# Attention's constant rows and first queries: which rows the products take, and which engine writes and loads them

## The chip, the cores and the metric

The kernel runs on one core of a Trainium2 chip. The metric is the device time of one execution in microseconds (us). Before the change it was 2974.33 us, the median of three runs (2973.43 to 2976.23). The engines are TensorE (PE; its weight loads are counted apart as PEld), VectorE (DVE), ScalarE (ACT), GpSimd (POOL) and SyncE (SP), which issues most of the DMA transfers.

## The reference: what is computed

One layer of a hybrid trunk over 2064 tokens (2048 and 16 meta tokens) of width 1024. One input projection feeds three groups side by side: an RG-LRU recurrence, a forgetting attention of 8 heads with 64 columns each, and an RWKV-7 recurrence. Their outputs are projected back, and a feed-forward layer of width 2816 follows. The change is in the attention, which is

```python
c = jnp.cumsum(log_f, axis=1).transpose(0, 2, 1)
...
s = jnp.einsum('bhqd,bhkd->bhqk', qb, kh).astype(jnp.float32) + (cb[..., :, None] - c[..., None, :])
s = jnp.where(kpos[None, :] <= qpos[:, None], s, -jnp.inf)
p = jax.nn.softmax(s, axis=-1)
return jnp.einsum('bhqk,bhkd->bhqd', p.astype(vh.dtype), vh)
```

`c` is the running sum of the logarithms of the forget gates; a score is a product of query and key, plus the difference of `c` at the two places.

## The kernel before

The program runs in stages: the input projection (products L177 to L179 into `psp`), with the recurrences taken in small steps beside it; then attention (class `Attn`); then the output projection (`pswo`), the feed-forward layer's two products (`psu`, `psd`). The last RWKV and RG-LRU blocks are not through when the projection ends, at about 860 us, so they lie beside the first attention heads. The names of these recurrence steps in the trace: `rwxu`, `rwrav`, `rwwa`, `rwgt`, `rww`, `rstate` are RWKV's tiles; L1330 and L1361 multiply with the state `rstate`, which DVE copies at L1334 for the next step of the chain, four times in a row for one block; L1366 follows it; `rwraw` (L1034) is a piece of the projection's output that SP loads for the next part, and L1044/L1045 (ACT, then DVE) mix it with its neighbour token.

The order in which each engine takes its instructions is decided by a scheduler, when the program is built, from the program's order and a model of the durations. On the chip each engine then takes its list strictly in that order, and SP's DMA issues too: an instruction that waits holds back everything behind it on its engine.

Attention runs over two halves, of the query blocks 0 and 1 and then 2 and 3 (512 queries each), and within a half over the 8 heads. Keys and queries are kept as a high and a low part. For one head and block:

- `keys()` (L521) loads with SP. `k1` holds the keys' high part in rows 0 to 63 and the low part in rows 64 to 127. `k2` holds the high part in rows 0 to 63 (L537), a row of ones in row 64, and the two parts of `c`, `ch` and `cl`, in rows 65 and 66 (L539, L540). The other rows are zeros.
- `maxima()` (L552) loads the queries with SP: `q3` (L563), `q1` twice (L564, L565), `q2` (L566). `q3` has zeros in row 64 and ones in rows 65 and 66. The product `mx` of `q3` and `k2` (L576) with the triangle of L578 gives scores, whose greatest value DVE finds for each query (L581, into `mc`, set by a memset at L569). They are brought into a row by transposes (L591), and ACT writes them into row 64 of `q2` (L592).
- `weights()` (L672) makes the scores in two products, `k1` with `q1` (L704) and `k2` with `q2` (L705), so that row 64 subtracts the maximum. ACT takes the exponential (L709), GpSimd cuts the triangle and adds up the sums (L711, L748), and the values are multiplied at L727.

Maxima have two banks in `mx()`, scores two. `q1`, `q2`, `q3` are rings of three tiles, `k1` and `k2` of two; a third `k2` is made by `rear()` when half 1 begins (L837 and on), in memory that the recurrences have left.

The constant rows of these tiles are written by `__init__` and `fixed()`: for a `q3` three DVE memsets (L491, L492, L493), for a `q2` one (L473), for a `k2` four DVE casts of 64 x 520 elements from a column of the identity matrix (L499). The meta tokens' own small attention, `meta()`, uses `fixed()` too, with eight rows of ones, and there GpSimd sets the keys' rows.

Of the kernel before, what the change touches and what calls it, by code (L numbers as in the profile page):

```python
# [8 lines left out]
F32 = mybir.dt.float32  # L9
# [23 lines left out]
class Core:  # L33


    def __init__(self, tc, ctx):
        self.tc = tc
        self.nc = tc.nc
        self.ctx = ctx
        self.uid = 0  # L40
        nc = self.nc
        self.const = ctx.enter_context(tc.tile_pool(name="const", bufs=1))
        self.ident = self.const.tile([P, P], F32, name="ident")
        make_identity(nc, self.ident[:])
        self.flip = 0
        self.root = self.apart = False
        self.turns = 0
# [315 lines left out]
KHALF = META + 8 * P  # L363
# [85 lines left out]
class Attn:  # L449
# [3 lines left out]


    ONES = 1

    def __init__(self, core, pool, psum, more, scr):
        self.core, self.pool, self.psum, self.more, self.scr = core, pool, psum, more, scr
        self.wide, self.bank, self.place, self.tail = False, 0, 0, False
        nc = self.nc = core.nc  # L460
        self.clock, self.later, self.serial, self.added = 0, [], 0, 0
        self.pending, self.loads, self.steps, self.beside = None, [], [], iter(())
        self.marks = {}


        self.turn = {"k": 1, "k2": 1, "q2": 0, "q3": 0}
        self.ring = {s: [] for s in self.turn}
        for i in range(self.AHEAD + 1):
            q3 = pool.tile([P, 512], F32R, tag=f"q3_{i}", name=core.n("q3"), bufs=1)
            self.fixed(q3, None, self.ONES)  # L470
            self.ring["q3"].append(q3)
            q2 = pool.tile([P, 512], F32R, tag=f"q2_{i}", name=core.n("q2"), bufs=1)
            nc.vector.memset(q2[64:128].bitcast(F32), 0.0)  # L473
            self.ring["q2"].append(q2)
            if i > 1:
                continue
            k1 = pool.tile([P, 2, KHALF], F32R, tag=f"k1_{i}", name=core.n("k1"), bufs=1)
            self.rear(pool, f"k2_{i}")
            v1 = pool.tile([P, 2, NKT // 2 + 1, 64], F32, tag=f"v1_{i}", name=core.n("v1"), bufs=1)
            self.ring["k"].append((k1, v1))  # L480

    def rear(self, pool, tag):
        k2 = pool.tile([P, 2, KHALF], F32R, tag=tag, name=self.core.n("k2"), bufs=1)
        self.fixed(None, k2, self.ONES)
        self.ring["k2"].append(k2)

    def fixed(self, q, k, ones):

        if q is not None:

            self.nc.vector.memset(q[64:128].bitcast(F32), 0.0)  # L491
            self.nc.vector.memset(q[64 : 64 + ones + 2].bitcast(F32), 1.0)  # L492
            self.nc.vector.memset(q[64 : 64 + ones].bitcast(F32), 0.0)  # L493
        if k is not None:
            if ones == 1:
                col = self.core.ident[64:128, 64:65]
                kf = k.rearrange("p h t -> p (h t)")
                for c in range(0, 2 * KHALF, KHALF // 2):
                    self.nc.vector.tensor_copy(kf[64:128, c : c + KHALF // 2], col.to_broadcast([64, KHALF // 2]))  # L499
            else:  # L500
                self.nc.gpsimd.memset(k[64:128].bitcast(F32), 0.0)
                self.nc.gpsimd.memset(k[64 : 64 + ones].bitcast(F32), 1.0)

    def next(self, s):
        self.turn[s] = (self.turn[s] + 1) % len(self.ring[s])
# [15 lines left out]
    def keys(self, h, nt):  # L521
# [15 lines left out]
        nc.sync.dma_start(k2f[0:64, :n], scr["kh"][r, :n])  # L537
        g = 64 + self.ONES
        nc.sync.dma_start(k2f[g : g + 1, :n], scr["ch"][h : h + 1, :n])  # L539
# [12 lines left out]
    def maxima(self, h, b, keys):  # L552

        nc, core, scr = self.nc, self.core, self.scr
        k1, k2, v1 = keys
        r = slice(64 * h, 64 * h + 64)
        t0, n, ref = META + 512 * b, 512, 4 * b
        qt = [(P * i, P, META + P * (4 * b + i)) for i in range(4)]
        ts = slice(t0, t0 + n)
        q3 = self.next("q3")  # L560
        q1 = self.t([P, 512], "q1", F32R, self.AHEAD + 1)
        q2 = self.next("q2")
        nc.sync.dma_start(q3[0:64, :n].bitcast(F32), scr["qh"][r, ts])  # L563
        nc.sync.dma_start(q1[0:64, :n].bitcast(F32), scr["qh"][r, ts])  # L564
        nc.sync.dma_start(q1[64:128, :n].bitcast(F32), scr["qh"][r, ts])  # L565
        nc.sync.dma_start(q2[0:64, :n].bitcast(F32), scr["ql"][r, ts])  # L566
        nq = len(qt)
        mc = self.t([P, 4, 5], "mc")
        nc.vector.memset(mc[:], NEG)  # L569
        for i, (qo, rows, prior) in enumerate(qt):  # L570
            for ci in range(len(MAX_CUTS) - 1):
                a, e = MAX_CUTS[ci], min(MAX_CUTS[ci + 1], prior + rows)
                if a >= e:
                    break
                ps, last = self.mx(), e == prior + rows
                nc.tensor.matmul(ps[:rows, : e - a], q3[:, qo : qo + rows], k2[:, a:e], start=True, stop=not last)  # L576
                if last:
                    nc.tensor.matmul(  # L578
                        ps[:rows, prior - a : e - a], core.identb[:], core.futureb[:], start=False, stop=True
                    )  # L580
                self.reduced = nc.vector.tensor_reduce(  # L581
                    mc[:rows, i, ci : ci + 1], ps[:rows, : e - a], axis=AX.X, op=ALU.max
                )
                yield None
        bias = self.t([P, NKT], "bias", bufs=self.AHEAD + 1)
        yield q1, q2, bias
        sh = self.t([P, 4], "sh")
        nc.vector.tensor_reduce(sh[:], mc[:], axis=AX.X, op=ALU.max)
        ps = self.mx()
        for i in range(nq):  # L590
            nc.tensor.transpose(ps[0:1, P * i : P * i + P], sh[:, i : i + 1], core.ident[:])  # L591
        nc.scalar.activation(q2[64:65], ps[0:1], AF.Identity, scale=-1.0, bias=core.ncref[:, ref, h : h + 1])  # L592
        nc.scalar.activation(
            bias[:], core.ccol[:, :, h], AF.Identity, scale=-1.0, bias=core.cref[:, ref, h : h + 1]
        )
        yield None
# [75 lines left out]
    def weights(self, h, b, keys, queries, fill):  # L672
# [6 lines left out]
        nc, core, scr = self.nc, self.core, self.scr  # L679
        k1, k2, v1 = keys  # L680
        q1, q2, bias = queries

        t0, n = META + 512 * b, 512
# [3 lines left out]
        ts = slice(t0, t0 + n)  # L687
# [4 lines left out]
        def group_scores(group):  # L692

            nonlocal done
            out = []
            for jj in range(0, len(group), 2):
                if done:
                    fill(min(1.0, (done + 2) / len(kt)))
                done += 2
                self.tick()  # L700
                for j, rows, c0, mw, mo in group[jj : jj + 2]:
                    w, ks = n - c0, P * j
                    ps = self.ps("sc", 2)
                    nc.tensor.matmul(ps[:rows, :w], k1[:, ks : ks + rows], q1[:, c0:n], start=True, stop=False)  # L704
                    self.scored = nc.tensor.matmul(  # L705
                        ps[:rows, :w], k2[:, ks : ks + rows], q2[:, c0:n], start=False, stop=True
                    )
                    p = self.pool.tile([P, 512], F32, tag="p", name=core.n("p"), bufs=self.NP)
                    last = nc.scalar.activation(p[:rows, :w], ps[:rows, :w], AF.Exp, bias=bias[:rows, j : j + 1])  # L709
                    if mw:  # L710
                        last = nc.gpsimd.affine_select(  # L711
                            out=p[:rows, :mw], in_=p[:rows, :mw], compare_op=ALU.is_ge, fill=0.0, base=mo,
                            pattern=[[1, mw]], channel_multiplier=-1,
                        )
                    out.append((p, last))
            return out
# [88 lines left out]
        for i, group in enumerate(groups):  # L805
            ps_ = group_scores(group)
            self.marks[h, b, i] = self.scored
            self.flush()
            self.pending = lambda a=(group, ps_, i == 0, i == len(groups) - 1): group_values(*a)
# [1614 lines left out]
```

## Time and profile before

| what | us |
|---|---|
| median of the runs | 2974.33 |
| time of the profiled execution | 2975.74 |
| its span, first to last instruction | 2974.0 |
| TensorE busy | 2852.4 |
| VectorE busy | 2039.5 |
| ScalarE busy | 1503.8 |
| GpSimd busy | 1285.9 |
| score products L704 and L705 start at | 873.70 and 884.52 |
| first reduce of maxima, L581 | 875.15 |
| first exponential, L709 | 885.40 |
| DVE's casts for the third k2 | 1094.9 to 1098.2 |

The mean granted clock of TensorE is 0.979 of its full speed. Times in rows are counted from the span's start. A row of a timeline or of the chain gives start, duration, engine, line and operation; a bracket behind it is the idle time just before it on its engine, with what ended it. A group's row gives count, least, median and greatest duration in ns, and the first and last start.

### The profile page before, as it was taken

What the parts mean: (1) busy time and instruction counts of PE and PEld (TensorE: products, weight loads), DVE (VectorE), ACT (ScalarE), POOL (GpSimd) and SP (SyncE); (2) the same over time, 40 slices, a digit from 0 to 9 for tenths busy, and PEclk for the clock granted to TensorE, in tenths of its full rate; (3) what the DMA queues carried; (4) which work ended last, traced back from release to release, by engine and by line L of the source; (5) the groups of instructions that cost most, each with busy time, mean ns of one, the idle gap of its engine ahead of it and who ended that gap; (6) DMA issues with size and microseconds to landing.
All of it is one profiled execution on the core that took longest, in us unless ns stands there. A gap on an engine that the chain in (4) does not pass through costs nothing.

```text
span 2974.0 us, 53306 instructions
## 1 busy us (share of the span) xinstructions
PE 2852.4 (96%) x18826; PEld 2444.3 (82%) x18826; DVE 2039.5 (69%) x3977; ACT 1503.8 (51%) x2937; POOL 1285.9 (43%) x1555
## 2 busy tenths in 40 slices
PE   6999999999988889999999999999999999999998
PEld 6998899888866555666568999999999999787887
DVE  5257754665677775566656998888778787646766
ACT  4246432554346655455644665666565665324333
POOL 1001121132114566667722667455655444646443
PEclk9999899999988999999999999999999999999999
DMA  6776479576653358445245665577777764436453
GB/s 216 237 231 220 144 250 320 182 245 218 217 125 81 88 116 229 106 98 136 64 130 189 203 193 175 165 230 211 208 211 219 218 198 138 150 114 221 146 173 121
DMA packets 470344, 530.52 MB, mean 178 GB/s; under 512 B 86862, under 2 KB 356888, under 8 KB 468524
## 3 DMA queue, kind: packets, MB, share of 16 engines
q1 hardware_dynamic: 469308, 526.18, 58.8%
q8 instruction: 148, 2.42, 0.3%
q14 instruction: 120, 0.98, 0.1%
q0 software_dynamic: 768, 0.93, 0.1%
HBM read 368.07 MB, written 158.90 MB: 177 GB/s over the span
## 4 chain that ended last, share of the span: by engine, by line
PE 75%; DVE 8%; DMA 7%; ACT 4%; issue 2%; POOL 2%; SPq 1%; DVEq 0%; POOLq 0%; ACTq 0%
PE psu L177 9%; PE psu L178 9%; PE psu L179 9%; PE psp L179 4%; PE psp L178 4%; PE psp L177 4%; PE psd L177 4%; PE psd L178 4%; PE psd L179 4%; PE po L727 4%; PE pswo L177 2%; PE pswo L178 2%; PE pswo L179 2%; PE sc L704 2%; PE mx L576 2%
## 5 line engine op out<-in xcount | busy, mean ns | idle before, releaser
L178 PE MATMUL psu<-xo,uw 128*128 128x344 f32 x1848 | 591.5, 320 | 0.0
L177 PE MATMUL psu<-xo,uw 128*128 128x344 f32 x1848 | 586.2, 322 | 2.4 <-DVE vb L1889 1.9
L179 PE MATMUL psu<-xo,uw 128*128 128x344 f32 x1848 | 582.0, 320 | 0.3 <-DVE uw L1698 0.3
L177 PE MATMUL psp<-xh,wh 128*128 128x384 f32 (+2 forms) x1152 | 378.7, 329 | 1.4 <-DMA wh<-scr_wk 1.0
L179 PE MATMUL psp<-xh,wl 128*128 128x384 f32 (+2 forms) x1152 | 376.8, 328 | 0.6 <-DMA wl<-scr_wk 0.6
L178 PE MATMUL psp<-xl,wh 128*128 128x384 f32 (+2 forms) x1152 | 375.3, 326 | 0.0
L1698 DVE TENSOR_TENSOR uw<-uq,uw 128x512 fp32r<-128x512 f32 x341 | 320.2, 944 | 59.1 <-ACT uw L1697 55.9
L177 PEld LDWEIGHTS psu<-xo,uw 128*128 128x128 f32 x1848 | 345.9, 188 | 4.2 <-DVE vb L1889 3.0
L178 PEld LDWEIGHTS psu<-xo,uw 128*128 128x128 f32 x1848 | 347.2, 188 | 0.0
L179 PEld LDWEIGHTS psu<-xo,uw 128*128 128x128 f32 x1848 | 345.7, 188 | 1.1 <-DVE uw L1698 1.1
L1697 ACT ACTIVATE uw<-uq 128x512 fp32r<-128x512 f32 x462 | 288.1, 627 | 94.8 <-PE psu L179 44.9
L709 ACT ACTIVATE p<-sc,bias 128x512 f32<-128x512 f32 (+4 forms) x352 | 197.5, 589 | 172.1 <-PE sc L705 142.1
L581 DVE TENSOR_REDUCE mc<-mx 128x1 f32<-128x512 f32 (+6 forms) x352 | 190.7, 567 | 116.7 <-PE mx L576 77.5
L1837 DVE SCALAR_TENSOR_TENSOR uy<-psu,ffn_cols,uy 128x342 f32<-128x342 f32 (+1 forms) x390 | 220.9, 568 | 60.3 <-ACT uy L1835 58.6
L1845 POOL TENSOR_TENSOR uy<-uy,uy 128x342 f32<-128x342 f32 (+1 forms) x132 | 145.1, 1099 | 232.5 <-DVE uy L1837 61.0
L1698 POOL TENSOR_TENSOR uw<-uq,uw 128x512 fp32r<-128x512 f32 x121 | 183.1, 1513 | 133.3 <-ACT uw L1697 111.9
L179 PEld LDWEIGHTS psp<-xh,wl 128*128 128x128 f32 x1152 | 218.6, 190 | 8.9 <-issue 6.2
L177 PEld LDWEIGHTS psp<-xh,wh 128*128 128x128 f32 x1152 | 218.4, 190 | 8.4 <-issue 4.4
L178 PEld LDWEIGHTS psp<-xl,wh 128*128 128x128 f32 x1152 | 218.3, 189 | 7.2 <-issue 5.7
L748 POOL TENSOR_TENSOR acc<-acc,p 128x512 f32<-128x512 f32 (+3 forms) x186 | 198.8, 1071 | 46.8 <-ACT p L709 21.3
L1698 DVE TENSOR_TENSOR fo<-u,fo 128x896 fp32r<-128x896 f32 x88 | 101.6, 1154 | 130.9 <-ACT fo L1697 130.3
L1697 ACT ACTIVATE fo<-u 128x896 fp32r<-128x896 f32 x88 | 81.3, 923 | 207.1 <-PE psd L179 116.0
(490 smaller groups left out, 6339.4 us busy)
## 6 DMA issues: line engine op xcount, KB each, us to landing
uq<-scr_us SPq DMA_DIRECT2D x220, 256.0 KB
uq<-in_ffn_up_dram SPq DMA_DIRECT2D x209, 256.0 KB
wl<-scr_wk SPq DMA_DIRECT2D x48, 512.0 KB
wh<-scr_wk SPq DMA_DIRECT2D x48, 512.0 KB
u<-scr_ff SPq DMA_DIRECT2D x88, 256.0 KB
scr_ff<-uy SPq DMA_DIRECT2D x110, 171.0 KB
raw<-in_w_in_dram SPq DMA_DIRECT2D x24, 512.0 KB
scr_wk<-wh SPq DMA_DIRECT2D x24, 512.0 KB
```

Source lines behind the costliest of these rows:

```text
L177: nc.tensor.matmul(out, ah, bh, start=first, stop=False, skip_group_check=more)
L178: nc.tensor.matmul(out, ah, bl, start=False, stop=False, skip_group_check=more)
L179: nc.tensor.matmul(out, al, bh, start=False, stop=last, skip_group_check=more)
L576: nc.tensor.matmul(ps[:rows, : e - a], q3[:, qo : qo + rows], k2[:, a:e], start=True, stop=not last)
L581: self.reduced = nc.vector.tensor_reduce(mc[:rows, i, ci : ci + 1], ps[:rows, : e - a], axis=AX.X, op=ALU.max)
L709: last = nc.scalar.activation(p[:rows, :w], ps[:rows, :w], AF.Exp, bias=bias[:rows, j : j + 1])
L727: mm = nc.tensor.matmul(po[at : at + 64, c0:n], v1[:rows, j], p[:rows, : n - c0], start=start and i < 2, stop=end and i + 2 >= len(group), ...
L748: eng.tensor_tensor(a, ps_[0][0][:rows, c0:n] if start and i == 1 else a, p[:rows, : n - c0], op=ALU.add)
L1697: core.nc.scalar.activation(hi, src, AF.Copy)
L1698: (eng or core.nc.vector).tensor_tensor(lo, src, hi, op=ALU.subtract)
L1837: core.conved = stt(y[:, :n], src[:, i : n + i], cw[:, 44 * i + cc : 44 * i + cc + 1], y[:, :n], op0=ALU.mult, op1=ALU.add)
L1845: core.pooled = nc.gpsimd.tensor_tensor(v[:, :n], g[:, :n], v[:, :n], op=ALU.mult)
```

## The change

1. The products L576 and L705 take only the rows in use: 67 (`MAXED`, keys, ones, `ch`, `cl`) and 65 (`SCORED`, keys and ones).
2. So the zeros in the other rows aren't needed. Of `q3` GpSimd sets rows 64 to 66 to one and then row 64 to zero; `q2` needs nothing, since ACT writes its row 64; of `k2` GpSimd sets row 64 to one. DVE sets none of these rows any more.
3. The third `k2` gets its row of ones from the first `k2`, by a DMA on SP.
4. For the first head's blocks 0 and 1 the four loads of the queries are issued by GpSimd instead of SP.
5. `fixed()` loses its branch for one row of ones. Only `meta()` calls it now, and it does there what it did.

```diff
     ONES = 1
+    SCORED = 64 + ONES
+    MAXED = SCORED + 2
...
             q3 = pool.tile([P, 512], F32R, tag=f"q3_{i}", name=core.n("q3"), bufs=1)
-            self.fixed(q3, None, self.ONES)
+            nc.gpsimd.memset(q3[64 : self.MAXED].bitcast(F32), 1.0)
+            nc.gpsimd.memset(q3[64 : self.SCORED].bitcast(F32), 0.0)
...
-            nc.vector.memset(q2[64:128].bitcast(F32), 0.0)
...
         k2 = pool.tile([P, 2, KHALF], F32R, tag=tag, name=self.core.n("k2"), bufs=1)
-        self.fixed(None, k2, self.ONES)
+        row = k2[64:65].bitcast(F32)
+        if len(self.ring["k2"]) < 2:
+            self.nc.gpsimd.memset(row, 1.0)
+        else:
+            self.nc.sync.dma_start(row, self.ring["k2"][0][64:65].bitcast(F32))
...
-            if ones == 1:
-                col = self.core.ident[64:128, 64:65]
-                kf = k.rearrange("p h t -> p (h t)")
-                for c in range(0, 2 * KHALF, KHALF // 2):
-                    self.nc.vector.tensor_copy(kf[64:128, c : c + KHALF // 2], col.to_broadcast([64, KHALF // 2]))
-            else:
-                self.nc.gpsimd.memset(k[64:128].bitcast(F32), 0.0)
-                self.nc.gpsimd.memset(k[64 : 64 + ones].bitcast(F32), 1.0)
+            self.nc.gpsimd.memset(k[64:128].bitcast(F32), 0.0)
+            self.nc.gpsimd.memset(k[64 : 64 + ones].bitcast(F32), 1.0)
...
-        nc.sync.dma_start(q3[0:64, :n].bitcast(F32), scr["qh"][r, ts])
...
+        queue = nc.gpsimd if h == 0 and b < 2 else nc.sync
+        queue.dma_start(q3[0:64, :n].bitcast(F32), scr["qh"][r, ts])
...
-                nc.tensor.matmul(ps[:rows, : e - a], q3[:, qo : qo + rows], k2[:, a:e], start=True, stop=not last)
+                r = slice(0, self.MAXED)
+                nc.tensor.matmul(ps[:rows, : e - a], q3[r, qo : qo + rows], k2[r, a:e], start=True, stop=not last)
...
-                        ps[:rows, :w], k2[:, ks : ks + rows], q2[:, c0:n], start=False, stop=True
+                        ps[:rows, :w], k2[: self.SCORED, ks : ks + rows], q2[: self.SCORED, c0:n], start=False, stop=True
```

The lines behind the edits are two further down in the changed kernel (L576 is L578, L581 is L583, L705 is L707, L1034 is L1036, L1045 is L1047, L1218 is L1220, L1334 is L1336).

The scheduler orders the instructions anew. The lists of all engines are alike up to about 862 us and, but for a few swaps, from about 1480 us on; between them they differ. DVE's list at the end of the input projection, first as it was (`rwix`, `rwe` and `rwbk` are tiles of the recurrence, `rps` a bank of its products; `q` and `k` are attention's tiles):

```order
L1195 COPY rwix_10072<-unit_1252 128x128 [waits DVE_49]
L491 MEMSET q_1422_11318 64x512
L473 MEMSET q_1423_11322 64x512
L499 CAST k_1425_11325<-ident 64x520 x4
L491 MEMSET q_1427_11331 64x512
L473 MEMSET q_1428_11335 64x512
L1109 SCALAR_TENSOR_TENSOR rwe_9814<-rwe_9814,rwk_9807 128x512 [waits DVE_49]
L1311 TENSOR_TENSOR rwgt_9401<-rps_9414,rwgt_9401 128x256 [waits PE_49]
L1312 TENSOR_TENSOR rwrav_7410<-rps_9414,rwrav_7410 128x4x64
L499 CAST k_1430_11338<-ident 64x520 x3
```

The first copy of `rstate` (L1334) stands nine rows behind this piece, and the first reduce of the maxima (L581) seven behind that copy. The same place in the changed kernel:

```order
L1197 COPY rwix_10072<-unit_1252 128x128 [waits DVE_49]
L570 MEMSET mc_11358 128x20
L570 MEMSET mc_11394 128x20
L1111 SCALAR_TENSOR_TENSOR rwe_9814<-rwe_9814,rwk_9807 128x512 [waits DVE_49]
L1313 TENSOR_TENSOR rwgt_9401<-rps_9414,rwgt_9401 128x256 [waits PE_49]
L1314 TENSOR_TENSOR rwrav_7410<-rps_9414,rwrav_7410 128x4x64
L1119 SCALAR_TENSOR_TENSOR rwbk_9909<-rwe_9814 128x8x64 [waits DVE_49]
L1336 COPY rstate<-rps_9426 128x128 [waits PE_49] x4
```

All four copies of the state now stand together, ahead of every reduce. The first reduces of the changed kernel come 27 rows further on, behind the recurrence's next part:

```order
L1047 SCALAR_TENSOR_TENSOR rwrav_9902<-rwraw_9903,rwkv_cols,rwrav_9902 128x4x64 [waits Activation_49]
...
L1381 TENSOR_TENSOR rww_961_7459<-rww_961_7459,rwgsm_9463 128x512 [waits DVE_49]
L1047 SCALAR_TENSOR_TENSOR rwwa_10603<-rwraw_10605,rwkv_cols,rwwa_10603 128x64 [waits DMAHW3_49,Activation_49]
L583 TENSOR_REDUCE mc_11358<-mx_11360 128x1 [waits PE_49]
L583 TENSOR_REDUCE mc_11358<-mx_11364 128x1 [waits PE_49]
```

They moved behind `rwwa`, which waits for a load of `rwraw`. That load is on SP. SP's list before, from the first key load of attention:

```order
L537 DMA k_1425_11325<-scr_kh 64x1040 [waits DMAHW2_49,PE_49]
L541 DMA k_1424_11324<-scr_kh 64x1040 [waits DMAHW3_49,PE_49]
L1218 DMA rwxu_10108<-dx_8878 16x8x16 [waits DMAHW4_49,Pool_49]
...
L539 DMA k_1425_11325<-scr_ch 1x1040 [waits DMAHW4_49,DVE_49]
L540 DMA k_1425_11325<-scr_cl 1x1040 [waits DMAHW5_49]
L542 DMA k_1424_11324<-scr_kl 64x1040 [waits DMAHW6_49]
L563 DMA q_1427_11331<-scr_qh 64x512 [waits DMAHW7_49]
```

Eight loads of `rwxu` stand there, then `ch`, which waits for DVE's rows, and the first query. The end of the same stretch in the changed kernel, behind the five loads of keys for each of the first two heads:

```order
L564 DMA q_1422_11318<-scr_qh 64x512 [waits DMAHW4_49]
L565 DMA q_1462_11454<-scr_qh 64x512 [waits DMAHW5_49,PE_49]
L566 DMA q_1462_11454<-scr_qh 64x512 [waits DMAHW6_49]
L567 DMA q_1423_11321<-scr_ql 64x512 [waits DMAHW7_49]
L545 DMA v_1426_11325<-scr_v 128x8x64 [waits DMAHW0_49]
L546 DMA v_1426_11325<-scr_v 16x64 [waits DMAHW1_49]
L545 DMA v_1426_11325<-scr_v 128x8x64 [waits DMAHW2_49]
L1036 DMA rwraw_10605<-scr_p 128x2x65 [waits DMAHW3_49,DVE_49]
L1220 DMA rwxu_10108<-dx_8878 16x8x16 [waits DMAHW4_49,Pool_49]
```

The four queries are those of the third block in turn; the first two blocks' are on GpSimd's list. The load of `rwraw`, which waits for DVE's second L1047 of `rwrav`, moved ahead of the eight loads of `rwxu`.

More of the change, by code (lines that the diff above doesn't have):

```diff
@@ L562, in maxima @@
         q2 = self.next("q2")
[L563 to L566, printed above, removed]
+        queue = nc.gpsimd if h == 0 and b < 2 else nc.sync
+        queue.dma_start(q3[0:64, :n].bitcast(F32), scr["qh"][r, ts])
+        queue.dma_start(q1[0:64, :n].bitcast(F32), scr["qh"][r, ts])
+        queue.dma_start(q1[64:128, :n].bitcast(F32), scr["qh"][r, ts])
+        queue.dma_start(q2[0:64, :n].bitcast(F32), scr["ql"][r, ts])
         nq = len(qt)
```

## The prediction

> **What bounds the kernel now.** The page's head, engine line and chain of waits come first.
>
> ```profile
> span 2974.0 us, 53306 instructions
> PE 2852.4 (96%) x18826; PEld 2444.3 (82%) x18826; DVE 2039.5 (69%) x3977; ACT 1503.8 (51%) x2937; POOL 1285.9 (43%) x1555
> PE 75%; DVE 8%; DMA 7%; ACT 4%; issue 2%; POOL 2%; SPq 1%; DVEq 0%; POOLq 0%; ACTq 0%
> ```
>
> TensorE is busy for 96% of the span, so nothing can be won but its idle time, 121.6 us, and time that it spends at a low clock. The view by stretches shows where attention lies (columns: stretch, length, then busy time and count of PE, its loads, DVE, ACT, POOL; then the granted clock, the DMA share and GB/s).
>
> ```profile
> 840.00:1240.00 400.00, 352.10 (x2770) 223.81 (x2771) 285.74 (x738) 211.95 (x446) 214.20 (x320) 0.90 0.50 123
> ...
> 1200.00:1260.00 60.00, 59.76 (x267) 37.90 (x266) 34.15 (x76) 28.91 (x56) 39.77 (x63) 0.96 0.48 113
> ...
> 860.00:870.00 10.00, 7.75 (x64) 5.05 (x62) 8.67 (x23) 0.35 (x2) 0.31 (x1) 0.66 0.44 100
> 870.00:880.00 10.00, 7.00 (x65) 5.49 (x65) 7.71 (x20) 0.00 (x0) 0.00 (x0) 0.51 0.79 200
> 880.00:890.00 10.00, 8.64 (x57) 6.24 (x55) 7.94 (x26) 5.00 (x12) 2.69 (x8) 0.50 1.13 214
> 890.00:900.00 10.00, 8.63 (x34) 5.62 (x34) 6.16 (x21) 3.68 (x7) 3.05 (x4) 0.62 0.85 173
> ```
>
> From 840 to 1240 TensorE is idle for 47.9 of 400 us; from 1200 on it is full. So the change can save or lose time only before about 1200, where the last recurrences and the first attention heads share the engines. At 860 to 900 two things meet: 8.0 us of idle PE (40 less 32.0), and a granted clock of 0.50 to 0.66.
>
> The chain of waits at that place (start, length, what):
>
> ```profile
> 862.35 0.48 DVE q L491
> ...
> 863.39 1.46 DVE k L499 x4
> ...
> 868.27 1.71 SPq L563
> ...
> 870.03 2.84 DMA q<-scr_qh
> ...
> 873.70 1.10 PE sc L704 x2
> ```
>
> The constant rows, SP's issue of the first query and its flight stand on the chain ahead of the first score. This is what the change touches.
>
> **Trimmed rows.** The products L576 and L705 take 67 and 65 rows in place of 128. Two products of equal width and different row counts follow one another (PE's timeline: start, busy, line, tile, rows, count):
>
> ```profile
> 880.12 1.12 PE L1361 MATMUL rps<-rstate,rwrav 64*64 64x64 f32 x16
> 881.17 1.12 PE L1366 MATMUL rps<-rww,rwsc 128*64 128x64 f32 x16
> ```
>
> 16 products of 64 rows took as long as 16 of 128. I take 0 us for all trimmed products; the same pair is the bound on either side.
>
> **Constants off VectorE.** Groups by line (count, durations min/median/max in ns, first and last start), then DVE's timeline behind them:
>
> ```profile
> L491 DVE MEMSET q<- x3: 485/485/485, 862.3 to 869.3; 64x512 f32 x3
> L473 DVE MEMSET q<- x3: 485/485/485, 862.9 to 869.9; 64x512 f32 x3
> L499 DVE CAST k<-ident x12: 358/428/1514, 863.4 to 1097.7; 64x520 fp32r<-64x520 f32 x12
> 871.79 0.28 DVE L1334 COPY rstate<-rps 128x128 f32<-128x128 f32 x1
> 875.15 0.85 DVE L581 TENSOR_REDUCE mc<-mx 128x1 f32<-128x144 f32 x2
> ```
>
> Six memsets are 2.9 us; eight of the twelve casts, by the chain's 1.46 for four, 2.9; six more memsets of 512 columns (L492 and L493, by the same 0.485) 2.9: some 8.7 us leave DVE before the first reduce. What waits for them is in PE's timeline (the bracket is the idle time before and its releaser):
>
> ```profile
> 867.13 0.45 PE L1330 MATMUL rps<-rstate,rwgt 64*64 64x64 f32 x6
> 872.13 0.38 PE L1330 MATMUL rps<-rstate,rwgt 64*64 64x64 f32 x2 [4.37 <-DVE rstate L1334]
> 873.70 1.10 PE L704 MATMUL sc<-q,k 128*128 128x512 f32 x2 [0.88 <-DMA q<-scr_qh]
> ```
>
> Without the constants the copy of the recurrence's state is late only by the products that it reads (L1330, done at 867.58). It starts at about 867.65 in place of 871.79: **−4.1 us** of the 4.37. What is late next is the chain of four state steps itself, some 1.1 us each (the copy's 0.28, eight products of which six took 0.45, and the handovers; an estimate).
>
> **GpSimd's side.** It gets three memsets of 3x512, three of 1x512, two of 1x2080 and eight DMAs. The nearest rows:
>
> ```profile
> 863.13 0.31 POOL L1215 MEMSET rwxu<- 128x256 f32 x1 [7.85 <-PE rps L1310]
> L1682 POOL MEMSET q<- 128x16 f32 x2 | 0.2, 120 | 4.1 <-DVE xo L1698 4.1
> L793 POOL DMA_DIRECT2D rb<-scr_rden x2: 537/544/552, 1501.5 to 1533.5; - x2
> rb<-scr_rden POOLq DMA_DIRECT2D x2, 128.0 KB, 2.7
> scr_p<-zeros POOLq DMA_DIRECT2D x12, 32.0 KB, 6.0
> ```
>
> 240 further elements per row cost 0.19 us, so a memset of 2080 is some 1.7 us and one of 512 some 0.5, estimates from these rows. Begun after the L1226 memset near 855, the five ahead of the loads (1.5 + 3.4) end near 860.3; five loads of 0.54 us are issued by 863, and land 2.7 to 6.0 us later, 865.7 to 869. The first score needs them after the four steps at about 874, so they have 5 us of slack, and the wait of 0.88 goes: **−0.9 us**. If the flight were doubled, 12 us, the price is 1 us. GpSimd's memset of rwxu (L1215) stands behind the five loads and moves from 863.13 to about 863.6: nothing waits for 0.5 us there.
>
> [...]
>
> **SP's side.** Eight loads leave SP (columns as in the chain; the line is the query's).
>
> ```profile
> 871.96 0.59 SPq L563 DMA_DIRECT2D q<-scr_qh  x1
> 884.12 0.53 SPq L1034 DMA_DIRECT2D rwraw<-scr_p  x1
> ```
>
> 8 × 0.59 is 4.7 us of issue time. The order shows what the scheduler puts there: the keys of the first two heads, a third query, values, and then L1036's rwraw load *ahead of* the eight rwxu loads. That load waits for DVE's second L1047 of rwrav. **This is the new wait**: behind it on DVE stand rwwa (L1047, waits for rwraw) and behind that the first max reduces L583, which before ran at 875.15, ahead of it.
>
> ```profile
> 881.28 0.91 ACT L1044 ACTIVATE rwrav<-rwraw,rwkv_om 128x256 f32<-128x256 f32 x2 [20.94 <-PE rps L1361]
> 882.49 0.88 DVE L1045 SCALAR_TENSOR_TENSOR rwrav<-rwraw,rwkv_cols,rwrav 128x256 f32<-128x256 f32 x2
> 884.12 4.21 DMA rwraw<-scr_p
> 885.40 1.17 ACT L709 ACTIVATE p<-sc,bias 128x512 f32<-128x512 f32 x2
> 888.35 0.35 ACT L1044 ACTIVATE rwwa<-rwraw,rwkv_om 128x64 f32<-128x64 f32 x1 [1.78 <-DMA rwraw<-scr_p]
> ```
>
> Worked forward: four steps from 867.65 end at 872.0, L1361's last row at 874.1, ACT's and DVE's parts (0.91, 0.88) at 876.0, rwraw lands 4.2 later at 880.2, rwwa is done near 881. The first reduce starts near 881 in place of 875.15, **6 us late**. TensorE has two banks for maxima and two for scores, and the exponentials need the maxima: with four such products and the rest of the recurrence's it has work until about 877, and I take it idle from there for **+4.5 us**; the bounds are 0 (the recurrence, whose rwraw load starts at 876 and not at 884, fills it) and 10 (the first exponential, 885.40 before, comes near 895, and nothing gives that back).
>
> **The third k2.** It is made when half 1 starts; chain, then PE's timeline:
>
> ```profile
> 1094.89 3.29 DVE k L499 x4
> ...
> 1099.49 4.40 DMA k<-scr_cl
> 1103.98 0.77 PE L576 MATMUL mx<-k,q 128*128 128x400 f32 x3 [1.68 <-DMA k<-scr_cl]
> ```
>
> The casts held back the loads of ch and cl, and TensorE waited 1.68 us for them. In the changed order SP copies the row and issues both without a wait on DVE: **−1.7 us**. Bounds: −5.0 (the 3.29 of DVE too, since reduces follow there) and +2.5 (the copied row, a load like the 4.40 one, could hold the same product).
>
> **Sum.** −4.1 − 0.9 − 1.7 + 4.5 = −2.2 us. The profiled execution's span is 2974.0 and its own time 2975.74, 1.74 around it and 1.41 above the median 2974.33 of the runs. Against the median: 2972.1, rounded **2972.0**. The rest of attention is reshuffled by the scheduler between 862 and about 1480, with the recurrence ahead of attention by more rows than before; its effect I take at nothing, with ±4 us, some third of the largest wait in TensorE's view of waits from 870 to 1200 (us, times, longest), which such shifts move:
>
> ```profile
> PE sc L704 <- ACT p L709: 13.5, 12, 2.6
> ```
>
> **The rivals.**
> 1. *Small gain or none* (the forecast): 2968.5 to 2980.2. For it: the freed wait and the new one lie in the same 15 us.
> 2. *The relief carries through.* The recurrence's 8 us of lead let its products fill the gap at 877, no new idle appears, and the casts' whole time is won at the third k2: −4.1 − 0.9 − 5.0 = −10, **2964**. For it: the chain runs through DVE's constants without a break from 862.35 to 865.9. Against it: it went on through SP and the queries, and PE's own stall was only 4.37 and 0.88.
> 3. *The queue on DVE decides (slower).* The reduces stand behind rwwa, attention begins 10 us late, and the recurrence's lead is worth nothing because attention's own work sets the end at 1200, with the waits for exponentials longer by their third: −6.7 + 10 + 4 = **+7, 2981**. It decides if TensorE's idle from 875 to 885 exceeds 7 us.
> 4. *The clock.* The stretch at 0.50 to 0.62 lasts from about 865 to 897. Each 10 us more or less of it at half speed are up to 5 us: **2967 or 2977**. A shorter first stall (0.3 for 4.37) speaks for less of it, the new idle at 877 for more, so I leave it at nothing. [...]
> 5. *The change does nothing*: were order and waits the same, 2974. The order says otherwise; it is inside rival 1.
>
> **How the numbers follow.** A measurement of this kernel can tell about 0.2%, 6 us. Forecast with its neighbours (1, 5 and the near ends of 4): 0.48. Rival 2 and the good end of 4: 0.31. Rival 3 and the bad end: 0.21. So faster 0.31, same 0.48, slower 0.21. The range for 8 in 10 leaves out some of both far ends: 2962 to 2981; the likeliest case's own is 2968.5 to 2980.2.
>
> **What would show it.** Right: DVE's first rstate copy near 867.7 and no 4 us wait ahead of L1332; query landings before 870; first L583 near 881 with PE idle ahead of it; no wait for scr_cl near 1100. Wrong: the first L583 before 877 (then rival 2), PE idle over 7 us at 875 to 885 (rival 3), a half clock that ends before 890 or after 905 (rival 4), or a score's second product that lasts otherwise than its first.

## The result: slower by 0.9%

| | median of runs, us | ratio to before, 95% interval |
|---|---|---|
| before, same sessions | 2978.35 | |
| changed | 3006.69 | 1.0087, 1.0063 to 1.0111 |

The profiled execution of the changed kernel took 3010.25 us. Its page (head, engines, chain by engine; the third line is TensorE's granted clock in 40 slices, in tenths):

```profile
span 3008.5 us, 53319 instructions
...
PE 2876.8 (96%) x18826; PEld 2457.6 (82%) x18826; DVE 2019.4 (67%) x3953; ACT 1506.1 (50%) x2937; POOL 1299.6 (43%) x1571
...
PEclk8999999999986888999999999999999999999999
...
PE 75%; DVE 7%; DMA 6%; ACT 5%; issue 3%; POOL 3%; SPq 2%; DVEq 0%; ACTq 0%; POOLq 0%
```

VectorE did lose its work (2019.4 us busy for 2039.5), but TensorE is busy for 24.4 us *longer* with the same 18826 products. The same work taking longer points to the clock, and the stretches of attention show one, first before the change, then after (columns as in the prediction; the clock is the third number from the end):

```profile
900.00:1000.00 100.00, 86.75 (x979) 58.69 (x978) 79.72 (x217) 65.09 (x151) 51.20 (x88) 0.91 0.33 80
1000.00:1100.00 100.00, 87.73 (x781) 55.05 (x771) 75.24 (x216) 61.08 (x131) 65.69 (x102) 0.95 0.45 105
1100.00:1200.00 100.00, 89.86 (x428) 49.40 (x430) 59.25 (x119) 47.29 (x87) 62.53 (x76) 0.92 0.73 195
```

```profile
900.00:1000.00 100.00, 90.49 (x928) 62.10 (x928) 72.14 (x218) 59.64 (x138) 43.68 (x77) 0.72 0.27 65
1000.00:1100.00 100.00, 88.99 (x713) 55.97 (x709) 66.71 (x192) 54.42 (x115) 60.09 (x94) 0.87 0.36 87
1100.00:1200.00 100.00, 84.03 (x384) 46.95 (x386) 48.90 (x111) 47.91 (x90) 62.49 (x82) 0.85 0.61 157
...
875.00:885.00 10.00, 3.68 (x29) 2.43 (x24) 7.26 (x25) 2.57 (x6) 0.00 (x0) 0.70 0.87 156
840.00:1240.00 400.00, 346.63 (x2737) 219.69 (x2735) 252.66 (x683) 200.75 (x422) 208.70 (x310) 0.82 0.49 119
```

Over 840 to 1240 the idle time of TensorE went from 47.9 to 53.4 us, 5.5 more. The clock went from 0.90 to 0.82, which over 400 us is 32 us less of full speed. Together that is near the 34.5 us by which the two profiled spans differ. It can be no more than near: half clock during idle time is counted in both, and this execution was 4.2 us later than the one before already ahead of the first changed place (GpSimd's memset of `rwxf`, below).

One stretch tells what kind of clock loss it is, 16 us inside the changed kernel's first heads:

```profile
912.00:928.00 16.00, 16.00 (x142) 10.97 (x143) 12.18 (x37) 12.14 (x23) 7.30 (x13) 0.50 0.09 23
```

TensorE had no idle time for 16 us, and stayed at half clock all the same. An idle time ahead may have brought the half clock (in e4, below, the clock was 1.00 from 40 to 50 and a mean 0.56 from 50 to 60, in the 13.49 us of idle time behind the first stream); that it stayed through 16 busy us points to the work itself. It need not be the trimmed products: among the 142 of the stretch are 64 of the recurrence with 32 rows (L1236, twice 32 in 1.07 us) and 32 with 64 rows (L1280, in 1.97 us). So this stretch is a hint, and the experiments have to decide.

### The profile page after: what moved, and what is told of

Same layout as the page of the kernel before. It is cut to its first block, busy times and chain, and to the rows that moved or that the text cites. A ratio compares the mean times of both kernels' runs of the same rounds, so it can differ in the third digit from the quotient of the medians.

```text
span 3008.5 us, 53319 instructions
## 1 busy us (share of the span) xinstructions
PE 2876.8 (96%) x18826; PEld 2457.6 (82%) x18826; DVE 2019.4 (67%) x3953; ACT 1506.1 (50%) x2937; POOL 1299.6 (43%) x1571
## 4 chain that ended last, share of the span: by engine, by line
PE 75%; DVE 7%; DMA 6%; ACT 5%; issue 3%; POOL 3%; SPq 2%; DVEq 0%; ACTq 0%; POOLq 0%
PE psu L177 9%; PE psu L178 9%; PE psu L179 9%; PE psp L179 4%; PE psp L178 4%; PE psp L177 4%; PE psd L177 4%; PE psd L178 4%; PE psd L179 4%; PE po L729 4%; PE pswo L177 2%; PE pswo L178 2%; PE pswo L179 2%; PE sc L706 2%; PE mx L578 2%
## 5 line engine op out<-in xcount | busy, mean ns | idle before, releaser
L583 DVE TENSOR_REDUCE mc<-mx 128x1 f32<-128x512 f32 (+5 forms) x352 | 190.2, 566 | 125.7 <-PE mx L578 87.0
```

Source lines behind the costliest of these rows:

```text
L583: self.reduced = nc.vector.tensor_reduce(mc[:rows, i, ci : ci + 1], ps[:rows, : e - a], axis=AX.X, op=ALU.max)
```

## The experiments

Two theories stood: **R**, that the clock granted to TensorE goes by the rows of the array that its products use, so that products of 65 and 67 rows do not bring the clock back; and **O**, that the new order and its waits cost the time. The ratios are to the kernel before, run on the same chip in the same session.

| run | rows | median, us | ratio, 95% interval | clock, 840 to 1260 |
|---|---|---|---|---|
| before | 128 | 2978.35 | | 0.90 |
| changed | 67, 65 | 3006.69 | 1.0087, 1.0063 to 1.0111 | 0.83 |
| e1 | 128 | 2989.80 | 1.0044, 1.0028 to 1.0060 | 0.89 |
| e2 | 128 | 2979.67 | 1.0011, 0.9997 to 1.0025 | 0.90 |
| e3, order of e2 | 67 | 2989.57 | 1.0047, 1.0032 to 1.0062 | 0.87 |
| e5 | 67, 65 | 3003.56 | 1.0089, 1.0062 to 1.0116 | 0.85 |
| e6 | 128 | 2988.52 | 1.0036, 1.0017 to 1.0056 | 0.91 |
| e7 | 128 | 2990.06 | 1.0050, 1.0030 to 1.0069 | 0.91 |
| e8, order of e7 | 67 | 3004.25 | 1.0091, 1.0065 to 1.0117 | 0.87 |
| e9 | 128 | 2981.09 | 1.0014, 0.9997 to 1.0032 | 0.91 |
| e10 | 128 | 2973.99 | 0.9997, 0.9985 to 1.0008 | 0.91 |
| e11 | 128 | 2976.63 | 0.9996, 0.9979 to 1.0014 | 0.91 |
| e12 | 67, 65 | 2994.53 | 1.0053, 1.0035 to 1.0070 | 0.85 |

The last column alone parts the runs: 0.89 to 0.91 wherever the products take 128 rows, 0.83 to 0.87 wherever they are trimmed, whatever the order.

**e4: the clock by itself.** Streams of products after idle times, with different rows:

```python
COLD = [(128,), (96,), (80,), (67,), (128, 67), (128, 67, 64), (64,)]   # each 120 products, rows in turn
WARM = [(128, 48), (67, 120), (64, 120), (32, 120)]                     # rows, count, without a gap
nc.tensor.matmul(ps[:], w[:r], m[:r], start=True, stop=True)            # 512 columns
```

> The computation is left out; the output is a copy of part of the input. TensorE runs streams of 120 products of 512 columns, each after an idle time of some 10 us, with 128, 96, 80, 67, 128 and 67 in turn, 128 67 64 in turn, and 64 rows; then 48 of 128 rows followed without a gap by 120 each of 67, 64 and 32 rows. Theory R: the streams of 128 rows go from half to full clock within some 8 us, those of 80, 67 and 64 rows stay at half clock to their end (0.43 us a product, 51 us a stream), the mixed ones lie between; at full clock 67 rows keep the clock. Theory O (rows don't count): all streams return to full clock alike, within 8 us.

PE's timeline of e4, one row a stream (the shape printed is that of a row's first product; the bracket is the idle time ahead), and then some stretches (without ACT, so the clock follows POOL):

```profile
16.22 30.14 PE L41 MATMUL ps<-m,w 128*128 128x512 f32 x120 [16.22 <-DVE m L34]
59.85 30.48 PE L41 MATMUL ps<-m,w 96*128 96x512 f32 x120 [13.49 <-DVE m L34]
103.82 51.54 PE L41 MATMUL ps<-m,w 80*128 80x512 f32 x120 [13.49 <-DVE m L34]
168.84 51.54 PE L41 MATMUL ps<-m,w 67*128 67x512 f32 x120 [13.49 <-DVE m L34]
233.87 30.84 PE L41 MATMUL ps<-m,w 128*128 128x512 f32 x120 [13.48 <-DVE m L34]
278.20 74.98 PE L41 MATMUL ps<-m,w 128*128 128x512 f32 x120 [13.49 <-DVE m L34]
366.66 51.54 PE L41 MATMUL ps<-m,w 64*128 64x512 f32 x120 [13.48 <-DVE m L34]
431.68 118.52 PE L47 MATMUL psw<-m,w 128*128 128x512 f32 x408 [13.48 <-DVE m L34]
```

```profile
10.00:20.00 10.00, 3.78 (x9) 3.01 (x10) 6.80 (x8) 0.00 (x0) 1.00 1.02 405
...
59.85:66.00 6.15, 6.15 (x17) 4.86 (x18) 1.76 (x1) 0.00 (x0) 0.60 0.00 0
66.00:90.33 24.33, 24.33 (x105) 19.21 (x103) 0.00 (x0) 0.00 (x0) 1.00 0.00 1
...
168.84:220.38 51.54, 51.54 (x120) 39.53 (x120) 1.76 (x1) 0.00 (x0) 0.50 0.00 0
...
430.00:440.00 10.00, 8.32 (x26) 6.66 (x27) 1.46 (x3) 0.00 (x0) 0.66 0.01 2
...
442.00:470.00 28.00, 28.00 (x121) 22.49 (x120) 0.00 (x0) 0.00 (x0) 1.00 0.00 1
470.00:504.00 34.00, 34.00 (x146) 26.35 (x145) 0.00 (x0) 0.00 (x0) 1.00 0.00 0
508.00:550.00 42.00, 42.00 (x99) 31.51 (x98) 0.00 (x0) 0.00 (x0) 0.50 0.00 0
```

The 96-row stream came back to full clock within about 6 us (0.60 over its first 6.15 us, then 1.00), and so did 128 and 67 in turn (mean 97.5 rows; 0.59 from 233.87 to 240.00, then 1.00). The streams of 80, 67 and 64 rows stayed at half clock (0.50) for all of their 51.5 us, at 0.43 us a product, without any idle time. The last stream came back with its 128-row products alone (mean clock 0.66 from 430 to 440, then 1.00). So did the first: its first nine products took 3.78 us, 0.42 each, which is the pace at half clock, and 43 took the next 10 us. Its clock column reads 1.00 from the start, so the column does not show the clock there. At full clock the 67-row and 64-row products kept it (1.00 from 442 to 504); the 32-row ones, which start near 501.6 (an estimate from the counts of the stretches), lost it soon after (mean 0.64 from 504 to 508, then 0.50). Both borders fit one estimate, worked out from these streams, the rows in use times the granted clock: at half clock the stream of 96 of 128 rows, 0.375 of the array's full rate, came back, and that of 80 rows, 0.31, did not; at full clock 64 rows (0.5) kept it and 32 (0.25) lost it. That is one execution, and only rows were varied; whether fewer columns count in the same way was not tried. A change between 128 and 67 rows has no price of its own here: the stream of both in turn took 30.84 us, that of 96 rows 30.48. So for these streams the clock went by the rows in use, as theory R says.

**e2 and e3, e7 and e8: the rows alone, in one order.** Trimming by itself makes the scheduler choose another order (e5), through the clock in its model of TensorE. Both pairs are put in order by a model with a clock that is always full; the twins then have the same lists on every engine.

```diff
+    TRN2Spec.PE_CLOCK = dataclasses.replace(TRN2Spec.PE_CLOCK, entry_columns=0.0)
...
-q3[:, qo : qo + rows], k2[:, a:e], start=True, stop=not last)
+q3[:67, qo : qo + rows], k2[:67, a:e], start=True, stop=not last)
-k2[:, ks : ks + rows], q2[:, c0:n], start=False, stop=True
+k2[:67, ks : ks + rows], q2[:67, c0:n], start=False, stop=True
```

> The kernel before with 128 rows, but put in order by a scheduler's model whose TensorE clock is always full, so that the order no longer hangs on the number of rows. Its own time says little (2960 to 3010 us); it is the base of its twin with 67 rows, which has the same order on every engine.

> The twin of e2 in the same order on every engine; the only difference is that both products take 67 rows instead of 128. Theory R: mean granted clock lower by 0.006 or more than e2's and time longer by 15 to 40 us. Theory O: within 6 us of e2, since no instruction has moved.

> e1 put in order by the model with a clock that is always full, as e2 was. Against e2 it differs by the moved constants and queries and by the order that they bring. If these moves cost by themselves: 2990 us or more. If e1's loss was that of one unlucky order: 2970 to 2982 us.

> The twin of e7 in the same order on every engine, with both products of 67 rows. Theory R: 8 to 25 us longer than e7, with a lower granted clock. Theory O: within 6 us of e7.

Measured: 9.9 us longer (e3 against e2) and 14.2 (e8 against e7), with nothing moved: from 870 to 1480 the traces of VectorE, ScalarE, GpSimd and SP agree row by row in each pair. The engine lines of e2, e3, e7 and e8 in turn:

```profile
PE 2850.5 (96%) x18826; PEld 2440.6 (82%) x18826; DVE 2037.1 (68%) x3977; ACT 1509.2 (51%) x2937; POOL 1288.0 (43%) x1555
PE 2865.5 (96%) x18826; PEld 2450.3 (82%) x18826; DVE 2038.6 (68%) x3977; ACT 1510.5 (51%) x2937; POOL 1284.8 (43%) x1555
PE 2852.4 (96%) x18826; PEld 2446.3 (82%) x18826; DVE 2030.6 (68%) x3953; ACT 1508.8 (51%) x2937; POOL 1303.8 (44%) x1579
PE 2865.2 (96%) x18826; PEld 2452.7 (82%) x18826; DVE 2036.5 (68%) x3953; ACT 1506.8 (50%) x2937; POOL 1297.5 (43%) x1579
```

TensorE is busy for 15.0 and 12.8 us longer with the same products, which is all of the 12.7 and 13.1 us by which the profiled spans differ. In 840 to 1260 the clock is lower by 0.03 and 0.04. So the rows cost time through the clock, and no order is needed for it. The sizes are less sure. The first pair is below the 15 us that R asked for, and its mean clock fell by 0.005 (0.979 to 0.974), not by 0.006; the second is inside R's range. By the scatter of the runs (means, 95%) the pairs differ by 9.4 ± 3.4 and 12 ± 10 us: both more than nothing, but Theory O's "within 6 us" is only just out in the first pair, and not by the second alone. e7 is 10 us over e2, just what it expected of moves that cost by themselves; but it is e1 in another order, with e1's longer memsets (below).

**e5: trimming alone.** The kernel before, only the two products trimmed.

> The kernel before, with only the products trimmed to 67 and 65 rows; constants stay on VectorE, queries on SP; the scheduler puts it in a new order. Theory R (trimmed products hold the clock at half): granted clock 0.975 or less, time 2987 to 3005 us. Theory O (the moved constants and queries cost it, rows nothing): within 6 us of the kernel before.

1.0089: trimming alone costs what the whole change costs. Its 27 us are more than the 10 to 14 of the twins, and e5 is in a new order too. Whether that order costs by itself or makes the trimmed rows dearer was not parted. With 128 rows a new order need not cost: e2, e10 and e11 have one each and can't be told from before.

**e1 and e6: full rows in the change.** GpSimd also writes the zeros; SP copies 64 rows for the third `k2`; in e6 the queries are back on SP.

```diff
-    SCORED = 64 + ONES
-    MAXED = SCORED + 2
+    SCORED = MAXED = 128
...
+            nc.gpsimd.memset(q2[64:128].bitcast(F32), 0.0)
...
+            self.nc.gpsimd.memset(rest, 0.0)
+            self.nc.gpsimd.memset(k2[64:65].bitcast(F32), 1.0)
```

> The changed kernel with all 128 rows in both products again: GpSimd sets the zeros too (q3 and q2 rows 64 to 127, k2 rows 64 to 127, same number of columns), and SP copies 64 rows for the third k2; queries stay on GpSimd's queue, nothing is on VectorE. Theory R (TensorE's clock gate counts the rows in use, so trimmed products keep the clock at half): the mean granted clock returns to 0.977 or more and the time to 2960 to 2985 us. Theory O (the reshuffled order with its waits ahead of the first maxima costs it): the order is still that of a change without VectorE's constants, so 2995 us or more. By the prediction's own sum, which gave the rows no part, it would be 2972.

> e1 (128 rows, constants on GpSimd) with the first queries back on SP's queue. If the rest of the loss, 13 us in e1, comes from the queries on GpSimd's queue: 2974 to 2982 us. If it comes from VectorE's constants being gone, so that the recurrence is put ahead of the first maxima: 2985 us or more, as e1.

The clock came back as R said, the time did not: e1 lies between the two theories' ranges, so there is a second cost, and e6, as long as e1, says that the queries' queue alone is not it. In both GpSimd writes each `k2` twice (in e1 1.83 us, then 1.82 or 1.83), so keys are ready late: the first values L731 came at 937 us in e1 and 919 in e6, against 899 before. So these are not the change with full rows; e9 was made for that.

**e9, e10, e12: rows and the place of the reduces, crossed.** In e9 each `k2` gets one memset as in the change (`rest` to 1.0; the zeros of `q3` and `q2` meet the unused rows). e10 is e9, and e12 the change, with

```diff
-        queue = nc.gpsimd if h == 0 and b < 2 else nc.sync
+        queue = nc.sync
```

By this edit the scheduler puts VectorE's first five reduces ahead of `rwwa` again.

> As e1, all 128 rows, but GpSimd writes nearly what it writes in the change: each k2 gets one memset (ones in rows 64 to 127 instead of row 64 alone; the zeros of q3 and q2 meet the rows that are not used), q3 one and q2 one short memset more. VectorE's first reduce of the maxima stands behind rwwa, 27 rows behind the state's copies, as in the change. So against the change the products' rows are nearly all that differs. If e1's first values at 937 us (899 before, 922 in the change) came from its longer memsets, this one starts by 925 and takes 2972 to 2984 us; if moving the constants costs by itself, 2985 us or more. Theory R: granted clock 0.976 or more.

> e9 with the first queries on SP's queue. Here the order has VectorE's first five reduces of the maxima ahead of rwwa, as before the change, and the constants off VectorE. If the reduces behind the wait for rwraw cost 4.5 us or more (the prediction's term), this is 4 to 10 us shorter than e9 and at 2965 to 2975 us; if the place of the reduces is worth nothing, within 3 us of e9.

> The changed kernel (67 and 65 rows) with the first queries back on SP's queue, nothing else; the order has VectorE's first five reduces ahead of rwwa, as in e10 and as before the change. It is e10 with trimmed products, as the change is e9 with trimmed products. If the rows and the place of the reduces add up: some 7 us shorter than the change (e9 less e10) and 20 to 28 us longer than e10, so 2994 to 3002 us, with a granted clock of 0.974 or less. If the rows harm only where the reduces come late: within 8 us of e10, 2974 to 2982 us.

VectorE's timelines of e9, then e10 (first state copy, then `rwwa` and the first reduce in their order):

```profile
873.15 0.29 DVE L1337 COPY rstate<-rps 128x128 f32<-128x128 f32 x1 [2.70 <-PE rps L1333]
...
886.68 0.28 DVE L1048 SCALAR_TENSOR_TENSOR rwwa<-rwraw,rwkv_cols,rwwa 128x64 f32<-128x64 f32 x1
889.13 0.65 DVE L584 TENSOR_REDUCE mc<-mx 128x1 f32<-128x144 f32 x2
```

```profile
867.65 0.29 DVE L1337 COPY rstate<-rps 128x128 f32<-128x128 f32 x1 [3.11 <-PE rps L1333]
...
874.40 0.64 DVE L584 TENSOR_REDUCE mc<-mx 128x1 f32<-128x144 f32 x2
...
877.58 0.27 DVE L1048 SCALAR_TENSOR_TENSOR rwwa<-rwraw,rwkv_cols,rwwa 128x64 f32<-128x64 f32 x1
```

From the state's copy to the first reduce it is 16.0 us in e9 and 6.8 in e10; the first values come at 926 and 897 us. e9 keeps its 2972 to 2984 and its clock (its first values are 1 us behind the 925 that it gave), and e10 is 7.1 us shorter by the medians (5 by the ratios), as expected of the prediction's term. The constants off VectorE cost nothing that can be told in e10. In time, all four, by the ratios:

| | 128 rows | trimmed | trimmed less full, of before |
|---|---|---|---|
| reduces behind `rwwa` | e9: 1.0014 | the change: 1.0087 | 0.73%, 22 us |
| reduces ahead of it | e10: 0.9997 | e12: 1.0053 | 0.56%, 17 us |
| behind less ahead | 0.17%, 5 us | 0.34%, 10 us | |

The middle figures nearly add up, and those of the trimming are two to three times the others. Two things limit this table. The intervals are wide: from those of the ratios, some ±9 and ±6 us on the 22 and 17, ±6 and ±9 on the 5 and 10. At full rows the place of the reduces is told from nothing only by the runs of e9 and e10 themselves, from one session: 6.7 ± 4.4 us. And the columns differ in more than rows, which the expectation of e9 overlooked: the scheduler made another order here too. From 870 to 1480, 75% of VectorE's instructions in the change stand in the order of e9, and 47% of those in e12 in the order of e10; for the twins it was all of them. So the 17 to 22 us are trimmed rows with the order that comes with them, and only the 10 to 14 of the twins are the rows by themselves. e12 lands inside the range given for adding up. The queries' queue and the place of the reduces change in one edit here, so the 5 to 10 us belong to the two together. e10, with all moves of the change but the queries and the trimming, is the fastest, and not to be told from before.

**e11: the third k2 alone.**

```diff
-        self.fixed(None, k2, self.ONES)
+        if len(self.ring["k2"]) < 2:
+            self.fixed(None, k2, self.ONES)
+        else:
+            self.nc.sync.dma_start(k2[64:128].bitcast(F32), self.ring["k2"][0][64:128].bitcast(F32))
```

> The kernel before with one edit: the third k2 gets its 64 constant rows by one DMA from the first k2 instead of four casts on VectorE. The prediction's term: 1.7 us shorter than before, between 5 shorter and 2.5 longer, and no wait of TensorE for scr_cl near 1104 us. If any edit of attention brings a new order that costs some microseconds whatever it does: 2980 us or more.

0.9996, 0.9979 to 1.0014: 1.7 us can't be told from nothing here, though an order that costs whatever the edit does (2980 us or more) is out. The wait for `scr_cl`, which was to be gone, is there in TensorE's waits of e11 from 1085 to 1160 (us, times, longest), and longer than the 1.68 before:

```profile
PE mx L579 <- DMA k<-scr_cl: 3.0, 1, 3.0
```

## Why the prediction was wrong, by its own steps

It forecast 2972.0 and a range of 2962 to 2981; the kernel takes 3006.69.

- **Trimmed rows: this step failed.** "I take 0 us for all trimmed products; the same pair is the bound on either side" is right of one product by itself. The changed kernel's own timeline has a full and a trimmed product of equal width side by side at one clock (1.00 from 946.0 to 947.2):

```profile
946.53 0.35 PE L706 MATMUL sc<-q,k 128*128 128x400 f32 x1
946.71 0.34 PE L707 MATMUL sc<-q,k 65*128 65x400 f32 x1
```

  The rows' price is in the clock, which the pair L1361 and L1366 could not show, since both ran at the same 0.50. Measured, the trimming costs 10 to 14 us in one order, and 17 to 27 with the orders that the scheduler makes for it (the crossed runs and e5).
- **Rival 4, the clock**, tied the half clock to idle time alone and priced it at 5 us either way. The granted clock of the changed kernel shows 32 us less of full speed. Its sign, a half clock that ends before 890 or after 905, did not show: the first stretch ended at 896 (granted clock 0.50 from 880 to 896, 1.00 from 896 to 904). The loss came in new stretches behind it, such as 912 to 928. Idle time is not all that counts: e4's 67-row stream was busy for 51.5 us without a gap and stayed at 0.50, where the 96-row stream was back at 1.00 within 6.15 us.
- **The state copy, −4.1: the wait went, as forecast.** Before, TensorE waited 4.37 us for it; what its end saved in time no run measured by itself. After (waits from 862 to 900):

```profile
PE rps L1388 <- DVE rww L1381: 6.3, 1, 6.3
PE rps L1392 <- DVE rww L1400: 2.1, 1, 2.1
PE rps L1312 <- ACT rww L1296: 1.9, 1, 1.9
PE rps L1332 <- DVE rstate L1336: 1.1, 3, 0.4
```

- **The new wait, +4.5: right in kind, somewhat small.** VectorE, SP and TensorE of the changed kernel:

```profile
870.85 0.29 DVE L1336 COPY rstate<-rps 128x128 f32<-128x128 f32 x1 [2.05 <-PE rps L1332]
...
877.21 0.48 DVE L1047 SCALAR_TENSOR_TENSOR rwrav<-rwraw,rwkv_cols,rwrav 128x256 f32<-128x256 f32 x1
...
883.71 0.28 DVE L1047 SCALAR_TENSOR_TENSOR rwwa<-rwraw,rwkv_cols,rwwa 128x64 f32<-128x64 f32 x1 [1.10 <-ACT rwwa L1046]
883.91 0.65 DVE L583 TENSOR_REDUCE mc<-mx 128x1 f32<-128x144 f32 x2
```

```profile
879.06 1.70 SPq L1036 DMA_DIRECT2D rwraw<-scr_p  x1
```

```profile
882.75 0.66 PE L1388 MATMUL rps<-ident,rww 128*128 128x128 f32 x2 [6.32 <-DVE rww L1381]
```

  VectorE took its list in order: the products and the triangle for the first reduces were done by 876.5 (L578 and L580), and yet VectorE was idle for 1.10 us until `rwwa` could run, with the first reduce behind it at 883.91. SP issued nothing from 877.20 to 879.06, when the load of `rwraw` went, and the loads of `rwxu` behind it in its list came from 880.86. The first reduce comes 13.1 us after the state's copy, 3.4 before the change; the forecast (881 less 867.65) had 13.3. That agreement is partly luck. From the copy to the end of `rwrav` it took 6.8 us where the prediction had 8.4 (a state step took 0.86 us, not 1.1), and from there to the end of `rwwa` 6.3 where it had 5; the two errors cancel. TensorE is idle for 6.3 of the 10 us from 875 to 885 (3.68 busy), under the 7 at which rival 3 would decide. With the second wait of 2.1 that is 8.4 us for 4.5. Crossed, the place of the reduces and the queries' queue are worth 5 us at full rows, 10 with trimmed ones, within the wide intervals given there. (GpSimd's memset of `rwxf`, ahead of the first changed place, comes at 859.19 in this execution and at 854.97 in the one before, so distances are compared.)
- **GpSimd's side: right, but for the flights.** A memset of 2080 columns took 1.82 us, one of 512 0.52, a load's issue 0.52 to 0.58. The queries landed 7.5 us after their issue (median; their low parts 9.4), more than the 2.7 to 6.0 taken, and so behind 870. The cover held: TensorE's waits from 862 to 900, above, have none for them. What made the flights longer was not tried.
- **The third k2, −1.7:** its wait is gone in the changed kernel, which has no wait for `scr_cl` between 1085 and 1160. Alone (e11) it gained nothing that can be told.
- **The sum.** Without trimming, e9 is at +0.14% (−0.03 to +0.32), some 4 us, against the −2.2 us of the sum; the terms on waits were off by a few microseconds. Of the 28 us by which the changed kernel is slower than before, the term of 0 takes 10 to 14 by itself, and 22 with the order that trimming brings. Another 4 us of the distance to the forecast lie in its base: it started from 2974.33, and the kernel before has 2978.35 in the sessions of the result.

## What to carry to other kernels

Rows of zeros took no time of their own in a product here (0.35 us with 128 rows, 0.34 with 65, at 400 columns), and they can pay for TensorE's clock: in e4 the streams of 80, 67 and 64 rows stayed at half clock for all of their 51.5 us, and that of 96 rows was back at full clock within 6.15 us. Before trimming an operand, read the granted clock of that stage, and count the rows that its products use over some microseconds, not busy time alone. And where a scheduler makes the order, compare twins in one order before a cost is put down to an edit.

## What was not expected of the hardware

The stream of e4 with 128, 67 and 64 rows in turn took 74.98 us for 120 products, 0.62 us each at a granted clock of 0.50, while those of 80, 67 and 64 rows alone took 0.43 us at the same clock. Changes between 128 and 67 alone had no such price (30.84 us for 120 products, at 1.00 from 240 us on). By an estimate, 74.98 less 51.54 us over 40 rounds, the changes to and from 64 rows cost 0.59 us for every three products at half clock; why was not tried.
